# A two-layer encoder: shorter norm columns, and weight splits whose VectorE half is emitted one step later

## The chip, the core and the metric

One core of one Trainium2 chip runs the whole kernel. Its engines work side by side, each through its own instructions in order: TensorE (PE; its weight loads are listed as PEld), VectorE (DVE), ScalarE (ACT), GpSimd (POOL), and SyncE (SP), which issues most transfers. The metric is device time in microseconds (us), lower is better. The chip is asked for 2.4 GHz on TensorE; the profile shows the granted share of that, 1.00 or 0.50 (1.2 GHz).

## The reference

Two layers over 544 tokens of width 1024 (512 tokens of a new stream, 32 of a running one), all in float32. A layer is

```
h = rmsnorm(x);  proj = h @ w_in                # 5792 columns: conv gates, latent q, latent kv, rope key, two gates
y_a = (b * causal_conv3(c * xin)) @ w_conv_out
q = rmsnorm(q_lat) @ w_uq;  c = rmsnorm(ckv);  k, v = c @ w_ukv
y_b = chunk_causal_attention(q, k, v) @ w_attn_out
x = x + rmsnorm((sigmoid(g_a)*y_a + sigmoid(g_b)*y_b) @ w_merge)
x = x + rmsnorm((silu(gate) * up) @ w_down)     # gate, up = rmsnorm(x) @ w_gate_up, width 2816
```

Each rmsnorm multiplies a token by 1/sqrt(mean of squares + eps) and by a gain for each channel.

## The kernel before

Channels lie on the 128 partitions and tokens in the free dimension, in two halves of 272 tokens (hf 0 and 1). TensorE multiplies in fp32r, so each operand is split into a rounded high part and a low remainder, and a product takes three matmuls (`mm3`, lines 184 to 186: low weight first, then low input, then high by high).

**Weights.** A weight tile of 128 x 1024 is loaded by SP into one of two `raw` buffers. `split` then makes the high half with a ScalarE cast (L129) and the low half with a VectorE subtraction (L130), which waits for the cast and is the last to read `raw`. The result is one `w` tile: one of a ring of three, or a large block where `gate` is given. One weight tile against one half is a unit of 24 matmuls (`dense`), called a unit below; the last third of the down projection has 18.

**Order.** SP, POOL and TensorE always run in the order in which the program emits. VectorE and ScalarE do so in the program-ordered stages: the first projection pass of layer 0, and everything from the merge projection of a layer to the end of the first projection pass of the next. Elsewhere (attention, convolution, the other projections) a planner orders these two, and `prep` splits weights on the spot.

**The feed.** In the program-ordered stages from the merge projection on, weights come from a list, `feed`. `load_next` starts a load; `split_next` splits the oldest loaded tile; `claim`, ahead of the unit that uses a tile, forces what is missing. `tick` is called after each unit, behind the instructions that evict it: it splits the oldest tile if it was loaded at least two ticks ago and its buffer or gate allows, and then loads one more tile if fewer than two are loaded and not split. The stages that draw on it are, in order: the merge projection `mg` (8 tiles for half 0, the same tiles again for half 1), gate and up `gu` (4 pairs for half 0, again for half 1, then 18 pairs with both halves in turn), down `dn` (three tiles for each m; m = 0 to 4 with both halves, then half 0 of m = 5, 6, 7 and half 1 of m = 7, 6, 5), and in layer 0 the first pass of the next layer, `in` (8 tiles for half 0, then again for half 1).

**Norms.** `Acc` and `Acc2` add up squares. `rsqrt_cols` turns them into token columns with one-column matmuls (L237, two instructions for each of three blocks of 128 tokens), forms 1/sqrt with an integer start and three Newton steps on VectorE (L242 to L246), and multiplies the identity by each column into diagonal tiles (L251). `bcast` multiplies a matrix of ones by such a tile (L259, six instructions), which gives the factor on all partitions. `post_chain` does the residual and the norms around it in steps that `dense` takes in the middle and at the end of a unit; it runs after the last unit of each half of `mg` and `dn`. There are 24 calls of `bcast`: 14 in layer 0 and 10 in layer 1. The norms of q and kv are taken for both halves at once by `qk_norms`, near the end of the first pass.

Of the kernel before, what the change touches and what calls it, by code (L numbers as in the profile page):

```python
# [11 lines left out]
ALU = mybir.AluOpType  # L12
AX = mybir.AxisListType

P = 128
NL = 2
T = 544
TH = 272
# [5 lines left out]
EPS = 1e-6  # L24
QSCALE2 = 96.0
# [3 lines left out]
TB3 = (0, 128, 144)  # L29
# [4 lines left out]
def kernel(  # L34
# [25 lines left out]
    pe, dve, act, pool = nc.tensor, nc.vector, nc.scalar, nc.gpsimd  # L60
# [22 lines left out]
    def small(shape, dt=F32, s="s"):  # L83
        return sp.tile(shape, dt, tag="s", name=nm(s))

    def tiny(shape, s="y"):
        return sp.tile(shape, F32, tag="y", name=nm(s), bufs=16)
# [21 lines left out]
    def f32(ap):  # L109
        return ap.bitcast(F32)  # L110

    ident = const.tile([P, P], F32, name="ident")
    ones = const.tile([P, P], F32, name="ones")
# [14 lines left out]
    def split(hi, lo, src, eng_hi=None):  # L128
        act.copy(hi, src)  # L129
        dve.tensor_sub(lo, src, f32(hi))  # L130
# [13 lines left out]
    pre = {}  # L144
# [8 lines left out]
    feed, loaded, free, now = [], [], [0], [0]  # L153

    def load_next():
        key, src, width, gate = feed.pop(0)
        raw = raw_tile()
        nc.sync.dma_start(raw[:, :width], src)
        loaded.append((key, raw, width, gate, now[0]))

    def split_next():
        key, raw, width, gate, _ = loaded.pop(0)
        w = w_tile(gate is not None)
        split(w[:, 0, :width], w[:, 1, :width], raw[:, :width])
        pre[key] = w
        if gate is None:
            free[0] -= 1

    def tick():
        now[0] += 1  # L170
        if loaded and loaded[0][4] <= now[0] - 2 and (loaded[0][3]() if loaded[0][3] is not None else free[0] > 0):
            split_next()
        if feed and len(loaded) < 2:
            load_next()

    def claim(key):
        while key not in pre:
            if not loaded:
                load_next()
            split_next()  # L180
        return pre.pop(key)

    def mm3(ps, whi, wlo, xhi, xlo, first, last):
# [47 lines left out]
    def rsqrt_cols(accs):  # L231
        n = 3 * len(accs)
        ps = psd(n)
        v = tiny([P, 12], "v")[:, :n]
        for i, (acc, scale, eps) in enumerate(accs):
            for b, o in enumerate(TB3):
                pe.matmul(ps[:, 3 * i + b : 3 * i + b + 1], lhsT=acc.t[:, o : o + P], rhs=ones[:, 0:1], start=True, stop=True)  # L237
        for i, (acc, scale, eps) in enumerate(accs):
            dve.tensor_scalar(v[:, 3 * i : 3 * i + 3], ps[:, 3 * i : 3 * i + 3], scale, eps, op0=ALU.mult, op1=ALU.add)
        y = tiny([P, 12], "y")[:, :n]  # L240
        t = tiny([P, 12], "t")[:, :n]
        dve.tensor_scalar(y.bitcast(I32), v.bitcast(I32), -0.5, float(0x5F3759DF), op0=ALU.mult, op1=ALU.add)  # L242
        for _ in range(3):
            dve.tensor_mul(t, y, y)
            dve.scalar_tensor_tensor(t, t, -0.5, v, op0=ALU.mult, op1=ALU.mult)
            dve.scalar_tensor_tensor(y, t, 1.5, y, op0=ALU.add, op1=ALU.mult)  # L246
        out = []
        for i in range(len(accs)):
            d = small([P, TH], s="dg")
            for b, (o, a) in enumerate(((0, 0), (P, 0), (2 * P, 112))):  # L250
                dve.tensor_scalar_mul(d[:, o : min(o + P, TH)], ident[:, a:P], y[:, 3 * i + b : 3 * i + b + 1])  # L251
            out.append(d)
        return out

    def bcast(d, tag="v"):
        ps = bank(tag)[:, :TH]
        for o in (0, P, 2 * P):
            e = min(o + P, TH)
            pe.matmul(ps[:, o:e], lhsT=ones, rhs=d[:, o:e], start=True, stop=True)  # L259
        return ps  # L260

    FS = 1.0 / (NC * P)
# [168 lines left out]
    with tc.manual_schedule(engines=VEC):  # L431
        raw, w = raw_tile(True), w_tile(False)
# [20 lines left out]
    for l in range(NL):  # L453
# [47 lines left out]
                if m < 5:  # L501
                    (accq if m < 3 else acck)[hf].add(dst)

        qk = []

        def qk_norms():
            qk.extend(rsqrt_cols([(acck[0], 1.0 / 256, EPS), (acck[1], 1.0 / 256, EPS),
                                  (accq[0], QSCALE2 / 384, EPS * QSCALE2), (accq[1], QSCALE2 / 384, EPS * QSCALE2)]))

        if l == 0:  # L510
            pend = []

            def evict(n):
                for _ in range(n):
                    p1_evict(*pend.pop(0))

            after = {
                (0, 0): lambda: w3(3),
                (1, 0): lambda: (next(norm_a), scale_b(0), w3(4)),
                (2, 0): lambda: (scale_b(1), w3(5)),  # L520
                (3, 0): lambda: (next(norm_a), w3(6), evict(2)),
                (4, 0): lambda: (w3(7), evict(2), scale_b(2)),
                (5, 0): lambda: (scale_b(3), evict(2)),
                (6, 0): lambda: (evict(1), next(norm_b)),
                (7, 0): lambda: evict(1),
                (1, 1): lambda: (next(norm_b), next(norm_a)),
                (3, 1): lambda: (next(norm_b), evict(4)),
                (4, 1): lambda: evict(1),
                (5, 1): lambda: evict(1),
                (6, 1): lambda: (evict(1), qk_norms()),  # L530
                (7, 1): lambda: (evict(1), next(norm_b)),
            }

            def w3(m):
                if m == 5:
                    nc.sync.dma_start(cosT, rope[0])
                    nc.sync.dma_start(sinT, rope[1])
                fetch(("in", 0, m), w_in[0, m], 1024, True, m in (4, 5))

            with tc.manual_schedule(engines=VEC):  # L540
                for m, hf, ps in win_tiles(range(8), 8, raws):
                    pend.append((m, hf, ps))
                    if (m, hf) in after:
                        after[(m, hf)]()
        else:
            pend = []
            for m, hf, ps in win_tiles(range(8), 8, P1Src(h, raws)):
                pend.append((m, hf, ps))
                if hf == 0 or hf in sready:
                    while pend:  # L550
                        p1_evict(*pend.pop(0))
                tick()
                if (m, hf) == (6, 1):
                    qk_norms()
            while 1 not in h:
                step()
            while loaded:
                split_next()
            vec.__exit__(None, None, None)
        wide[0] = False  # L560

# [410 lines left out]
        def tail(units, key, widths, rhs, l, post_key, pre_l, pre_key, x_src, x_dst, gaps, outs):  # L972
            mres = [blk([P, NC, TH], F32, "m") for _ in range(2)]
            accs = [Acc(), Acc()]
            ws = {}
            left = [NC, NC]
            for n, (m, hf) in enumerate(units):
                left[hf] -= 1
                ps = psd(TH)
                for pi, wdt in enumerate(widths):  # L980
                    if (m, pi) not in ws:
                        ws[(m, pi)] = claim((key, m, pi))
                    dense(ps, ws[(m, pi)], rhs(hf, pi), wdt // P, first=pi == 0, last=pi == len(widths) - 1)
                    if (m, 1 - hf) not in units[n + 1 :] or (m, hf) == (5, 0) and len(widths) > 1:
                        del ws[(m, pi)]
                        if key == "mg" and m < 3 or key == "dn" and m != 6:
                            free[0] += 1
                    if pi < len(widths) - 1:
                        tick()
                done.add((key, m, hf))  # L990
                if accs[hf].q:
                    accs[hf].merge()
                accs[hf].square(ps)
                act.mul(mres[hf][:, m, :], ps, g(l, post_key, m))
                if left[hf] == 0:
                    accs[hf].merge()
                if (key, m, hf) == ("mg", 0, 1):
                    act.activation(tiny([P, 1]), ones[:, 0:1], AF.Silu)
                tick()
                if left[hf] == 0:  # L1000
                    xb = blk([P, NC, TH], F32, "xb")
                    for q in range(NW):
                        nc.gpsimd.dma_start(pair(xb, q), pair(x_src(hf), q))
                    chains.append(post_chain(pre_l, pre_key, mres[hf], accs[hf], xb, x_dst(hf), gaps[hf], hf, **outs[hf]))
# [29 lines left out]
        for _ in range(3):  # L1034
            load_next()
            split_next()
        load_next()
        now[0] += 1
        units = [(m, hf) for hf in range(2) for m in range(8)]
# [163 lines left out]
```

## Time and profile before

| | us |
|---|---|
| median of three runs | 2024.89 (2022.95 to 2026.08) |
| the profiled execution | 2026.63 |
| its span, first to last instruction | 2024.6 |
| TensorE busy | 1992.8 |
| VectorE busy | 1147.1 |
| ScalarE busy | 827.2 |

Busy time of TensorE is taken from matmul records whose ends are modelled and overlap. How long a stretch really takes is read from the distance between starts.

### The profile page before, as it was taken

How to read it: one execution, taken by the hardware profiler on the slowest of the kernel's cores; microseconds unless marked ns; L12 is line 12 of the kernel's file. 1: busy time of each engine (PE TensorE's matmuls, PEld its weight loads, DVE VectorE, ACT ScalarE, POOL GpSimd, SP SyncE). 2: the span in 40 equal slices, each digit the busy share in tenths (PEclk: the TensorE clock that was granted, in tenths of full speed). 3: DMA queues.
4: the chain of work that ended last, by engine and by line, in shares of the span. 5: the costliest groups of instructions: out<-in, count | busy, mean ns of one | idle time of the engine just before them, and what ended most of it. 6: DMA issues, size and time to landing. Idle time of an engine off the chain costs nothing.

```text
span 2024.6 us, 37375 instructions
## 1 busy us (share of the span) xinstructions
PE 1992.8 (98%) x15588; PEld 1970.8 (97%) x15588; DVE 1147.1 (57%) x2410; ACT 827.2 (41%) x1676; POOL 85.7 (4%) x212
## 2 busy tenths in 40 slices
PE   8999999999999999999999999999999999999997
PEld 8999999999999999999999999999999999999997
DVE  7877776534467444422668777864344664444234
ACT  5455555622353223222444555556123533222231
POOL 0100000000000000000100100100000000000000
PEclk9999999999999999999999999999999999999998
DMA  5122222222342222232532222222223412222233
GB/s 192 62 77 68 69 82 69 92 97 84 116 150 84 84 84 84 84 97 86 184 105 77 65 65 75 88 83 88 84 94 118 158 55 93 85 95 81 79 115 125
DMA packets 58890, 190.92 MB, mean 94 GB/s; under 512 B 7969, under 2 KB 9665, under 8 KB 58593
## 3 DMA queue, kind: packets, MB, share of 16 engines
q1 hardware_dynamic: 49104, 163.58, 24.1%
q0 software_dynamic: 8320, 22.66, 3.4%
q8 instruction: 122, 2.00, 0.4%
q10 hardware_dynamic: 1296, 2.29, 0.3%
q14 instruction: 48, 0.39, 0.1%
HBM read 174.11 MB, written 10.20 MB: 91 GB/s over the span
## 4 chain that ended last, share of the span: by engine, by line
PE 93%; DVE 4%; DMA 1%; ACT 1%; issue 1%; SPq 0%; DVEq 0%; ACTq 0%
PE ps_d L184 16%; PE ps_d L186 16%; PE ps_d L185 16%; PE ps_s L184 7%; PE ps_s L186 7%; PE ps_s L185 7%; PE ps_t L184 6%; PE ps_t L186 6%; PE ps_t L185 6%; PE ps_t L757 2%; DMA raw<-in_w_in 1%; PE ps_v L772 1%; PE ps_v L773 1%; DVE w L130 1%; ACT w L129 1%
## 5 line engine op out<-in xcount | busy, mean ns | idle before, releaser
L130 DVE TENSOR_TENSOR w<-raw,w 128x1024 fp32r<-128x1024 f32 (+4 forms) x317 | 363.8, 1148 | 433.5 <-ACT w L129 432.5
L129 ACT CAST w<-raw 128x1024 fp32r<-128x1024 f32 (+4 forms) x317 | 312.1, 986 | 263.3 <-PE ps_d L186 109.4
L184 PE MATMUL ps_d<-hh,w 128*128 128x272 f32 x1080 | 314.9, 292 | 1.3 <-DVE v L130 1.3
L185 PE MATMUL ps_d<-hl,w 128*128 128x272 f32 x1080 | 312.0, 289 | 0.8 <-DVE hl L314 0.8
L186 PE MATMUL ps_d<-hh,w 128*128 128x272 f32 x1080 | 312.1, 289 | 0.0
L184 PE MATMUL ps_d<-gh,w 128*128 128x272 f32 x704 | 205.9, 292 | 6.0 <-DVE w L130 6.0
L184 PEld LDWEIGHTS ps_d<-hh,w 128*128 128x128 f32 x1080 | 203.8, 189 | 3.0 <-PE ps_d L186 1.7
L185 PEld LDWEIGHTS ps_d<-hl,w 128*128 128x128 f32 x1080 | 203.5, 188 | 2.0 <-DVE hl L314 1.3
L186 PE MATMUL ps_d<-gh,w 128*128 128x272 f32 x704 | 204.5, 291 | 0.0
L185 PE MATMUL ps_d<-gl,w 128*128 128x272 f32 x704 | 203.5, 289 | 0.0
L186 PEld LDWEIGHTS ps_d<-hh,w 128*128 128x128 f32 x1080 | 203.1, 188 | 0.0
L184 PEld LDWEIGHTS ps_d<-gh,w 128*128 128x128 f32 x704 | 133.3, 189 | 6.5 <-DVE w L130 6.3
L184 PE MATMUL ps_s<-gh,w 128*128 128x272 f32 x464 | 136.9, 295 | 1.1 <-DVE w L130 1.1
L186 PE MATMUL ps_s<-gh,w 128*128 128x272 f32 x464 | 136.1, 293 | 0.0
L185 PE MATMUL ps_s<-gl,w 128*128 128x272 f32 x464 | 135.4, 292 | 0.0
L185 PEld LDWEIGHTS ps_d<-gl,w 128*128 128x128 f32 x704 | 133.6, 190 | 0.0
L186 PEld LDWEIGHTS ps_d<-gh,w 128*128 128x128 f32 x704 | 133.3, 189 | 0.0
L184 PE MATMUL ps_t<-gh,w 128*128 128x272 f32 x432 | 125.5, 290 | 0.0
L186 PE MATMUL ps_t<-gh,w 128*128 128x272 f32 x432 | 125.0, 289 | 0.0
L185 PE MATMUL ps_t<-gl,w 128*128 128x272 f32 x432 | 124.3, 288 | 0.0
L1051 ACT ACTIVATE sl<-sl 128x272 f32<-128x272 f32 x88 | 38.0, 432 | 183.2 <-DVE sl L1050 182.0
L1059 ACT CAST fh<-sl 128x272 fp32r<-128x272 f32 x88 | 36.9, 420 | 162.1 <-DVE sl L1057 162.1
(330 smaller groups left out, 5410.0 us busy)
## 6 DMA issues: line engine op xcount, KB each, us to landing
raw<-in_w_in SPq DMA_DIRECT2D x91, 512.0 KB, 3.2
raw<-in_w_gu SPq DMA_DIRECT2D x88, 512.0 KB, 3.2
raw<-in_w_mix SPq DMA_DIRECT2D x48, 512.0 KB, 3.2
raw<-in_w_dn SPq DMA_DIRECT2D x36, 512.0 KB, 3.5
raw<-in_w_dn SPq DMA_DIRECT2D x18, 384.0 KB, 3.0
raw<-in_w_b SPq DMA_DIRECT2D x16, 320.0 KB, 2.8
x_mid<-xb POOLq DMA_DIRECT2D x16, 272.0 KB, 2.3
xb<-x_mid POOLq DMA_DIRECT2D x16, 272.0 KB, 4.4
```

What stands on the lines that cost most here:

```text
L129: act.copy(hi, src)
L130: dve.tensor_sub(lo, src, f32(hi))
L184: pe.matmul(ps, lhsT=wlo, rhs=xhi, start=first, stop=False)
L185: pe.matmul(ps, lhsT=whi, rhs=xlo, start=False, stop=False)
L186: pe.matmul(ps, lhsT=whi, rhs=xhi, start=False, stop=last)
L757: pe.transpose(pt[:, o * P : o * P + P], probs[qt][:, kt * P : kt * P + P], ident)
L772: pe.matmul(out, lhsT=both, rhs=ptl[:, b, o : o + 256], start=kt == 0, stop=False)
L773: pe.matmul(out, lhsT=both, rhs=pth[:, b, o : o + 256], start=False, stop=kt == nkt - 1)
L1051: act.activation(sl, sl, AF.Silu)
L1059: act.copy(fh[:, i % 8, :], sl)
```

## The change

The diff has two halves. The norm half: `rsqrt_cols` takes two refinement steps, the first of higher order (seven instructions in place of nine), with other constants, and returns the columns themselves; no diagonal tiles are made; `bcast` transposes each column, read as 128 equal columns, with `pe.transpose`, three instructions in place of six; and `qk_norms` is called once for each half (layer 0 after units (4,1) and (6,1), layer 1 after (2,1) and (6,1)). The split half: in the feed, `split_next` emits only the ScalarE cast and puts the tile into `half`; `finish`, called at the head of the next tick or by `claim`, emits the VectorE subtraction. A tile in `half` counts against the limit of two in `tick`. The ticks inside the last unit group of a `tail` are left out.

```
     def split_next():
         key, raw, width, gate, _ = loaded.pop(0)
         w = w_tile(gate is not None)
-        split(w[:, 0, :width], w[:, 1, :width], raw[:, :width])
-        pre[key] = w
+        act.copy(w[:, 0, :width], raw[:, :width])
+        half.append((key, raw, w, width))
         if gate is None:
             free[0] -= 1
 
+    def finish():
+        while half:
+            key, raw, w, width = half.pop(0)
+            dve.tensor_sub(w[:, 1, :width], raw[:, :width], f32(w[:, 0, :width]))
+            pre[key] = w
+
     def tick():
         now[0] += 1
+        finish()
         if loaded and loaded[0][4] <= now[0] - 2 and (loaded[0][3]() if loaded[0][3] is not None else free[0] > 0):
             split_next()
-        if feed and len(loaded) < 2:
+        if feed and len(loaded) + len(half) < 2:
             load_next()
 
     def claim(key):
         while key not in pre:
-            if not loaded:
-                load_next()
-            split_next()
+            if not half:
+                if not loaded:
+                    load_next()
+                split_next()
+            finish()
         return pre.pop(key)
...
-        for _ in range(3):
-            dve.tensor_mul(t, y, y)
-            dve.scalar_tensor_tensor(t, t, -0.5, v, op0=ALU.mult, op1=ALU.mult)
-            dve.scalar_tensor_tensor(y, t, 1.5, y, op0=ALU.add, op1=ALU.mult)
-        out = []
-        for i in range(len(accs)):
-            d = small([P, TH], s="dg")
-            for b, (o, a) in enumerate(((0, 0), (P, 0), (2 * P, 112))):
-                dve.tensor_scalar_mul(d[:, o : min(o + P, TH)], ident[:, a:P], y[:, 3 * i + b : 3 * i + b + 1])
-            out.append(d)
-        return out
-
-    def bcast(d, tag="v"):
+        dve.tensor_mul(t, y, y)
+        dve.tensor_mul(t, t, v)
+        dve.scalar_tensor_tensor(u, t, -10.0 / 3.0, t, op0=ALU.add, op1=ALU.mult)
+        dve.scalar_tensor_tensor(y, u, 5.0, y, op0=ALU.add, op1=ALU.mult)
+        dve.tensor_mul(t, y, y)
+        dve.scalar_tensor_tensor(t, t, -27.0 / 1024.0, v, op0=ALU.mult, op1=ALU.mult)
+        dve.scalar_tensor_tensor(y, t, 0.5625, y, op0=ALU.add, op1=ALU.mult)
+        return [y[:, 3 * i : 3 * i + 3] for i in range(len(accs))]
+
+    def bcast(y, tag="v"):
         ps = bank(tag)[:, :TH]
-        for o in (0, P, 2 * P):
-            e = min(o + P, TH)
-            pe.matmul(ps[:, o:e], lhsT=ones, rhs=d[:, o:e], start=True, stop=True)
+        for b, o in enumerate(TB3):
+            pe.transpose(ps[:, o : o + P], y[:, b : b + 1].to_broadcast([P, P]), ident)
         return ps
...
-        def qk_norms():
-            qk.extend(rsqrt_cols([(acck[0], 1.0 / 256, EPS), (acck[1], 1.0 / 256, EPS),
-                                  (accq[0], QSCALE2 / 384, EPS * QSCALE2), (accq[1], QSCALE2 / 384, EPS * QSCALE2)]))
+        def qk_norms(hf):
+            qk[hf], qk[2 + hf] = rsqrt_cols([(acck[hf], 1.0 / 256, EPS), (accq[hf], QSCALE2 / 384, EPS * QSCALE2)])
...
-                    if pi < len(widths) - 1:
+                    if pi < len(widths) - 1 and n < len(units) - 1:
                         tick()
```

## Rows read from the trace of the kernel before

**Rows 1.** The page: busy time by engine, share of the span, instructions.

```profile
PE 1992.8 (98%) x15588; PEld 1970.8 (97%) x15588; DVE 1147.1 (57%) x2410; ACT 827.2 (41%) x1676; POOL 85.7 (4%) x212
```

**Rows 2.** Waits of PE: releaser, us in total, times, longest.

```profile
PE ps_v L259 <- DVE dg L251: 5.5, 2, 2.8
...
PE ps_d L237 <- DVE acc L224: 2.4, 2, 1.5
...
PE ps_d L185 <- DVE hl L314: 0.8, 2, 0.4
```

**Rows 3.** Waits of DVE, the first.

```profile
DVE w L130 <- ACT w L129: 432.5, 238, 9.9
```

**Rows 4.** Timeline of PE around a broadcast and a run of transposes: start, us, instruction.

```profile
583.78 0.73 PE L259 MATMUL ps_v<-dg,ones 128*128 128x128 f32 x6
584.36 0.37 PE L184 MATMUL ps_s<-mh,w 128*128 128x272 f32 x1
...
112.28 0.93 PE L757 MATMUL ps_t<-ident,pr 128*128 128x128 f32 x7
112.97 0.37 PE L184 MATMUL ps_d<-hh,w 128*128 128x272 f32 x1
```

**Rows 5.** Windows: stretch, us, busy time by engine, granted clock (PEclk), DMA share, GB/s.

```profile
61.90:65.30 3.40, 3.40 (x17) 3.40 (x16) 3.16 (x18) 0.00 (x0) 0.00 (x0) 0.50 0.00 0
1020.40:1024.40 4.00, 1.16 (x10) 0.97 (x10) 3.62 (x17) 2.02 (x5) 0.00 (x0) 1.00 0.58 206
1024.14:1028.76 4.62, 4.62 (x28) 4.62 (x27) 4.62 (x7) 1.24 (x2) 0.00 (x0) 0.63 0.43 138
1066.46:1072.05 5.59, 5.59 (x25) 5.59 (x26) 4.47 (x27) 0.00 (x0) 0.00 (x0) 0.50 0.00 0
```

**Rows 6.** Timeline of DVE at the end of the kernel.

```profile
2014.39 0.29 DVE L251 TENSOR_SCALAR dg<-ident,y 128x128 f32<-128x128 f32 x1
```

**Rows 7.** Timeline of PE at the end of the kernel.

```profile
2014.82 1.43 PE L259 MATMUL ps_v<-dg,ones 128*128 128x128 f32 x6 [2.63 <-DVE dg L251]
```

**Rows 8.** Timeline of ACT in the merge projection of layer 0.

```profile
554.56 0.40 ACT L215 ACTIVATE sq<-ps_s 128x272 f32<-128x272 f32 x1 [1.61 <-PE ps_s L186]
554.86 0.48 ACT L994 ACTIVATE m<-ps_s,gn 128x272 f32<-128x272 f32 x1
555.23 1.05 ACT L129 CAST w<-raw 128x1024 fp32r<-128x1024 f32 x1
557.59 0.40 ACT L215 ACTIVATE sq<-ps_t 128x272 f32<-128x272 f32 x1 [1.32 <-PE ps_t L186]
```

**Rows 9.** Timeline of DVE there.

```profile
556.31 1.23 DVE L130 TENSOR_TENSOR w<-raw,w 128x1024 fp32r<-128x1024 f32 x1 [2.07 <-ACT w L129]
...
563.56 0.43 DVE L224 TENSOR_TENSOR acc<-acc,sq 128x272 f32<-128x272 f32 x1
```

**Rows 10.** The page: weight loads, KB each, median us from issue to landing.

```profile
raw<-in_w_mix SPq DMA_DIRECT2D x48, 512.0 KB, 3.2
```

**Rows 11.** Timeline of ACT near the end of half 0 of the down projection of layer 0.

```profile
966.54 1.05 ACT L129 CAST w<-raw 128x1024 fp32r<-128x1024 f32 x1 [1.81 <-DMA raw<-in_w_dn]
...
971.55 0.40 ACT L215 ACTIVATE sq<-ps_s 128x272 f32<-128x272 f32 x1 [1.16 <-PE ps_s L186]
```

**Rows 12.** Timeline of ACT in the first pass of layer 1.

```profile
1017.30 0.38 ACT L500 COPY lat<-ps_s 128x272 f32<-128x272 f32 x1
1017.71 0.43 ACT L215 ACTIVATE sq<-lat 128x272 f32<-128x272 f32 x1
```

**Rows 13.** Timeline of DVE there.

```profile
1019.75 1.23 DVE L130 TENSOR_TENSOR w<-raw,w 128x1024 fp32r<-128x1024 f32 x1 [1.09 <-ACT w L129]
1020.89 0.15 DVE L239 TENSOR_SCALAR v<-ps_d 128x3 f32<-128x3 f32 x1
...
1028.45 0.72 DVE L335 TENSOR_TENSOR m<-m,ps_v 128x544 f32<-128x544 f32 x1
```

**Rows 14.** Timeline of PE there.

```profile
1023.48 0.81 PE L259 MATMUL ps_v<-dg,ones 128*128 128x128 f32 x6 [2.84 <-DVE dg L251]
```

More of the change, by code (lines that the diff above doesn't have):

```diff
@@ L159, in load_next @@
         loaded.append((key, raw, width, gate, now[0]))
+    half = []
     def split_next():
@@ L241, in rsqrt_cols @@
         t = tiny([P, 12], "t")[:, :n]
+        u = tiny([P, 12], "u")[:, :n]
         dve.tensor_scalar(y.bitcast(I32), v.bitcast(I32), -0.5, float(0x5F3759DF), op0=ALU.mult, op1=ALU.add)
-        for _ in range(3):
-            dve.tensor_mul(t, y, y)
-            dve.scalar_tensor_tensor(t, t, -0.5, v, op0=ALU.mult, op1=ALU.mult)
-            dve.scalar_tensor_tensor(y, t, 1.5, y, op0=ALU.add, op1=ALU.mult)
-        out = []
-        for i in range(len(accs)):
-            d = small([P, TH], s="dg")
-            for b, (o, a) in enumerate(((0, 0), (P, 0), (2 * P, 112))):
-                dve.tensor_scalar_mul(d[:, o : min(o + P, TH)], ident[:, a:P], y[:, 3 * i + b : 3 * i + b + 1])
-            out.append(d)
-        return out
-    def bcast(d, tag="v"):
+        dve.tensor_mul(t, y, y)
[7 more added lines that the diff above has]
+    def bcast(y, tag="v"):
         ps = bank(tag)[:, :TH]
-        for o in (0, P, 2 * P):
-            e = min(o + P, TH)
-            pe.matmul(ps[:, o:e], lhsT=ones, rhs=d[:, o:e], start=True, stop=True)
+        for b, o in enumerate(TB3):
+            pe.transpose(ps[:, o : o + P], y[:, b : b + 1].to_broadcast([P, P]), ident)
         return ps
@@ L502, in p1_evict @@
                     (accq if m < 3 else acck)[hf].add(dst)
-        qk = []
-        def qk_norms():
-            qk.extend(rsqrt_cols([(acck[0], 1.0 / 256, EPS), (acck[1], 1.0 / 256, EPS),
-                                  (accq[0], QSCALE2 / 384, EPS * QSCALE2), (accq[1], QSCALE2 / 384, EPS * QSCALE2)]))
+        qk = {}
+        def qk_norms(hf):
+            qk[hf], qk[2 + hf] = rsqrt_cols([(acck[hf], 1.0 / 256, EPS), (accq[hf], QSCALE2 / 384, EPS * QSCALE2)])
         if l == 0:
@@ L527 @@
                 (3, 1): lambda: (next(norm_b), evict(4)),
-                (4, 1): lambda: evict(1),
+                (4, 1): lambda: (evict(1), qk_norms(0)),
                 (5, 1): lambda: evict(1),
-                (6, 1): lambda: (evict(1), qk_norms()),
+                (6, 1): lambda: (evict(1), qk_norms(1)),
                 (7, 1): lambda: (evict(1), next(norm_b)),
@@ L552 @@
                 tick()
+                if (m, hf) == (2, 1):
+                    qk_norms(0)
                 if (m, hf) == (6, 1):
-                    qk_norms()
+                    qk_norms(1)
             while 1 not in h:
@@ L558 @@
                 split_next()
+            finish()
             vec.__exit__(None, None, None)
@@ L1036 @@
             split_next()
+        finish()
         load_next()
```

## The prediction, made before the changed kernel was run

> **What bounds the kernel now.** Read the busy times first: TensorE is busy for 1992.8 of 2024.6 us, with 15588 matmuls [rows 1]. Everything else matters only where TensorE waits, runs at the lower clock, or is given more or fewer instructions. So read its waits second. Those that the change touches are small: 5.5 us in two waits for the diagonal tiles of a norm (2.8 the longest), 2.4 for the summed squares in front of a norm, 0.8 for the low half of a normed input [rows 2]. Third, VectorE: it waits 432.5 us for ScalarE's cast in front of the weight subtraction [rows 3]. That is the wait at which the split half aims, but on an engine that is idle for over 40% of the span it is worth only what TensorE loses by it. Fourth, the windows with the granted clock: it is 0.50 in 61.90 to 65.30 and in 1066.46 to 1072.05, both behind the 24 one-column matmuls of the q and kv norms, and falls behind 1020.40 to 1024.40, where TensorE was busy for 1.16 us of 4.00 [rows 5].
>
> A unit of 24 matmuls takes 3.03 us (two evictions, 554.56 and 557.59, [rows 8]), 0.126 each.
>
> **Norm half, broadcast.** Six instructions took 583.78 to 584.36, 0.58 us; seven transposes took 112.28 to 112.97, 0.10 each [rows 4], so three take 0.30. The trace has no transpose that reads one column 128 times over. If that read costs nothing the gain is 0.28, and if it eats the gain it is 0. I take 0.28, from the nearest row. Of the 24 calls one lies in the tail; 23 x 0.28 = 6.4 us off TensorE's own time (bounds 0 to 6.4). The Trainium skill ("TensorE: Matmul & The Clock Gate", Part 4: PE-mode transpose) says that a 128 x 128 transpose took about 275 ns in one kernel. Paid three times over, that would be 0.83 per broadcast, and the term 23 x 0.25 = 5.8 us lost instead of 6.4 gained; the 0.10 between starts in [rows 4] speaks against that reading.
>
> **Norm half, VectorE.** Two small instructions (0.2 each) and three diagonal tiles for each norm go. In the tail nothing covers them: the first diagonal tile starts at 2014.39 [rows 6] and TensorE at 2014.82 [rows 7], of which 0.3 goes; with 0.4 for the two and half of the 1.43 of the broadcast, 1.4 us. In layer 0 the twelve diagonal tiles of the q and kv norms stand on VectorE ahead of the normed input that TensorE awaits; those 0.8 us [rows 2] go. Elsewhere VectorE's saving lies beside matmuls and is worth nothing.
>
> **Norm half, clock.** The 24 one-column matmuls become 12 and 12, some units apart. Six of them with the 1.5 us wait in front [rows 2], near 1015, did not lower it (1.00 in 1020.40 to 1024.40, [rows 5]), so I take it that 12 don't. What comes back: a unit that took 5.59 us at 0.50 (1066.46, layer 1) takes 3.03, 2.6; in 61.90 to 65.30 there ran 17 matmuls in place of 27 [rows 5], 10 x 0.126 = 1.3. The third fall cost one unit 4.62 - 3.03 = 1.6 [rows 5] and goes with its wait (below). Sum 5.5, bounds 0 and 5.5.
>
> **Split half, the supply.** This is where I differ from what the edit says. A `raw` tile now counts against the limit of two until its subtraction is emitted. Before, a tick split one tile and loaded one: a tile per tick. Now follow it: a tick that casts A still counts A and B, and loads nothing; the next finishes A, casts B, loads C; the next finishes B and loads D, but casts nothing, because C is only one tick old. Two tiles in three ticks. Where both halves use a tile in turn (`gu`, most of `dn`) the demand is one in two, and I found casts at the same tick as before or with two units to spare. Three stretches ask for one tile per tick.
>
> *Place n* is the point ahead of unit n. Merge, half 0: tiles 5, 6, 7 were cast at places 3, 4, 5; now at 4, 5 and 7. The cast at place 7 stands on ScalarE behind the eviction of unit 6, and unit 7 on TensorE behind both halves. The price from [rows 8, 9]: square to cast 0.67 (554.56 to 555.23), cast to subtraction 1.08 (556.31), subtraction 1.23, and some 0.2 for the last matmul to drain: 3.2 us of idle TensorE. Tiles 5 and 6, cast one unit ahead, need 3.2 against the unit's 3.03: 0.2 late. The loads themselves are no bound: they take 3.2 us [rows 10] and start as soon as a buffer is free. 3.4 per layer, 6.8.
>
> Down, m = 6 and 7 of half 0 (six tiles, places 0 to 5): cast before at -2, -1, 0, 1, 2, 3, now at -1, 1, 2, 3, 4, 5. Before, the cast of (7,0) could start at 966.54, ahead of the eviction at 971.55 [rows 11]; now it stands behind that eviction: 3.2 again. (6,1) is 0.2 late; (7,1) and (7,2) have no eviction in front. 3.4 per layer, 6.8.
>
> First pass of layer 1, half 0: tiles 1 to 7 were cast at places -4 to 2, and now, with the inner ticks of the last units gone too, at 0, 1, 3, 4, 5, 6, 7. Tile 1: 0.3. Tile 2: its subtraction now stands on VectorE behind the sum of the unit just ended: 0.2 + 0.38 copy + 0.43 square [rows 12] + 0.44 sum + 1.23 [rows 9] = 2.7. Tile 3: 0.2 + 0.38 + 0.41 + 1.05 + 1.23 = 3.3. Tiles 4 and 5 the same with one 0.72 instruction of the post chain in front [rows 13]: 4.0 each. Tiles 6 and 7 have no square in front: 2.9 each. Sum 20.1. Against that goes what is lost there now: the column arithmetic at 1020.89 stood behind a subtraction at 1019.75 [rows 13], so TensorE waited 2.84 at 1023.48 [rows 14], and 1.5 for the squares [rows 2]: 4.3. Net 15.8.
>
> **Clock behind the new waits.** Each long wait is like 1020.40 to 1024.40, after which one unit lost 1.6. Ten such waits give 0 to 16 us; I take 7 (3 of the 4 lone ones, 4 of the 6 in the pass), 11.2.
>
> **The sum.** + 6.8 + 6.8 + 15.8 + 11.2 - 5.5 - 6.4 - 0.8 - 1.4 = + 26.5 us. The profiled execution took 2026.63 (span 2024.6 and 2.0 around it), 1.7 above the median of 2024.89; on the median that is 2051.4, so 2051. With the bounds of clock and broadcast: 2036 to 2062.
>
> **Rivals.** (1) *The feed never runs dry*, because casts are not held behind evictions and the two-in-three rate never decides. For it: the casts in [rows 11] do run ahead. Against: in [rows 8] the cast follows the eviction. The gains stand alone, 6.4 + 0.8 + 1.4 + 5.5 + 4.3 = 18.4: 2006. It decides if TensorE shows no wait for L129's tile at place 7 of the merge. (2) *Only the pass starves*; the four lone waits are covered: 26.5 - 13.6 - 4.8 = 8.1, 2033. (3) *The clock stays at 0.50 through the starved pass*, since TensorE works less than half of it: six units lose 2.6 each in place of 6.4 in all, and all four lone waits lose 1.6: + 37, 2062. (4) *As (2), and no clock falls in the pass*: + 1.7, about 2026, no change.
>
> **Chances.** Mine 0.56, (1) 0.14, (2) 0.12, (3) 0.12, (4) 0.06. Within 0.2% (4 us) is what a measurement can't tell from no change. Faster 0.14, same 0.06, slower 0.80. The range takes in (2) and most of (3): 2028 to 2063; the likeliest case's own is 2036 to 2062.
>
> **What would show it.** TensorE's waits for the weight subtraction rise to some 30 us, with waits of about 3 us ahead of the eighth merge unit and the 37th of the down projection in each layer, and six ahead of units of layer 1's first pass; broadcasts last 0.30; the clock is full behind the q and kv norms and falls in the first pass. If those long waits are missing, the supply argument is wrong and the time is near 2006; if they are there and the total is under 2030, the clock term or the gains are mis-sized.

## The result and the profile after

The changed kernel took 2055.65 us (median of 4 runs, 2054.06 to 2059.71) against 2024.72 for the kernel before (4 runs, 2022.95 to 2026.08): ratio 1.0156 with the interval 1.0139 to 1.0174, 30.9 us slower. The profiled execution took 2054.99 us, its span is 2053.0, 28.4 more than before. Its lines have moved: the three matmuls of a product are L195 to L197, the feed's cast is L166 and its subtraction L174, the subtraction of a split in one piece L130, the broadcast L267, the columns' sums L248.

The page's busy times answer to [rows 1], and the two groups of VectorE's subtractions (busy us, mean ns, idle before and what ended it) to [rows 3].

```profile
PE 1994.3 (97%) x15516; PEld 1969.1 (96%) x15516; DVE 1126.3 (55%) x2318; ACT 825.3 (40%) x1676; POOL 86.1 (4%) x212
...
L174 DVE TENSOR_TENSOR w<-raw,w 128x1024 fp32r<-128x1024 f32 (+1 forms) x168 | 199.7, 1192 | 209.0 <-ACT w L166 208.9
L130 DVE TENSOR_TENSOR w<-raw,w 128x1024 fp32r<-128x1024 f32 (+4 forms) x149 | 163.0, 1094 | 138.5 <-ACT w L129 137.2
```

TensorE is busy 1.5 us longer and idle 26.9 us longer (span less busy: 58.7 against 31.8). VectorE's wait for the casts did fall, from 432.5 to 208.9 + 137.2 = 346.1. So the loss is TensorE's waiting, and what the norm half saved has to have been eaten inside the busy time. The waits of TensorE in the kernel after (releaser, us in total, times, longest) say for what it waits:

```profile
PE ps_d L195 <- DVE w L174: 13.8, 5, 3.7
PE ps_s L195 <- DVE w L174: 8.7, 3, 3.1
PE ps_t L195 <- DVE w L174: 8.5, 3, 3.1
...
PE ps_v L267 <- DVE y L261: 1.9, 1, 1.9
...
PE ps_d L196 <- DVE hl L322: 0.8, 2, 0.4
PE ps_d L196 <- DVE qn L130: 0.8, 1, 0.8
```

Eleven waits, 31.0 us, for the weight subtraction of the feed. Before there were none of this kind: TensorE's waits for a weight subtraction (6.0 and 1.1 us) all lie in the first 13 us, outside the feed. Those for the broadcast's operand fell from 5.5 to 1.9, the tail's; the low half in layer 0 is as it was; a wait for `qn` in the attention of layer 0 is new. The timeline of TensorE (start, us, instruction, in brackets the idle time before it) has four of the eleven by themselves, alike in both layers: in front of the eighth merge unit (573.52, 1601.42) and of the 37th unit of the down projection (976.09, 2003.99). In the first pass of layer 1 seven follow each other.

```profile
573.52 0.39 PE L195 MATMUL ps_t<-mh,w 128*128 128x272 f32 x1 [3.06 <-DVE w L174]
...
976.09 0.39 PE L195 MATMUL ps_d<-fh,w 128*128 128x272 f32 x1 [3.06 <-DVE w L174]
...
1017.31 0.39 PE L195 MATMUL ps_d<-hh,w 128*128 128x272 f32 x1 [1.38 <-DVE w L174]
...
1023.80 0.39 PE L195 MATMUL ps_s<-hh,w 128*128 128x272 f32 x1 [2.55 <-DVE w L174]
...
1030.23 0.39 PE L195 MATMUL ps_t<-hh,w 128*128 128x272 f32 x1 [2.80 <-DVE w L174]
...
1037.20 0.59 PE L195 MATMUL ps_d<-hh,w 128*128 128x272 f32 x1 [3.68 <-DVE w L174]
...
1046.02 0.59 PE L195 MATMUL ps_s<-hh,w 128*128 128x272 f32 x1 [3.13 <-DVE w L174]
...
1053.50 0.60 PE L195 MATMUL ps_t<-hh,w 128*128 128x272 f32 x1 [2.68 <-DVE w L174]
...
1061.99 0.40 PE L195 MATMUL ps_d<-hh,w 128*128 128x272 f32 x1 [2.68 <-DVE w L174]
```

By the distance from the last matmul's start to the next one's, less the usual 0.126, each lone wait costs 3.22 us, and those of the pass cost 1.54, 2.71, 2.97, 3.84, 3.32, 2.84 and 2.98, together 20.2.

Why a lone wait lasts 3.2 us is read from ScalarE ahead of 573.52. It answers to [rows 8], where the tile that was cast at 555.23 was one needed later; here unit 7 itself awaits the tile cast at 571.17.

```profile
570.50 0.40 ACT L226 ACTIVATE sq<-ps_s 128x272 f32<-128x272 f32 x1 [2.25 <-PE ps_s L197]
570.80 0.48 ACT L1004 ACTIVATE m<-ps_s,gn 128x272 f32<-128x272 f32 x1
571.17 1.04 ACT L166 CAST w<-raw 128x1024 fp32r<-128x1024 f32 x1
```

The cast stands behind the eviction of the unit just ended, the subtraction (572.24, 1.22 us) behind the cast, and TensorE behind both. In the pass the chain is the same with the in-order queues of both engines in it. Tile 3 on VectorE: the subtraction stands behind a chain instruction (as [rows 13] had one) and a sum, and then waits another 0.41 us for its cast, so here the cast still decides:

```profile
1027.46 0.72 DVE L343 TENSOR_TENSOR m<-m,ps_v 128x544 f32<-128x544 f32 x1 [3.71 <-PE ps_v L267]
1028.10 0.43 DVE L235 TENSOR_TENSOR acc<-acc,sq 128x272 f32<-128x272 f32 x1
1028.95 1.22 DVE L174 TENSOR_TENSOR w<-raw,w 128x1024 fp32r<-128x1024 f32 x1 [0.41 <-ACT w L166]
```

The windows (us, busy times, granted clock, DMA share, GB/s) answer to [rows 5]: the clock is full where the q and kv norms now lie, and falls behind three of the four lone waits (575.00, 1602.40, 2005.20; not behind 976) and behind four of the pass.

```profile
59.00:66.00 7.00, 7.00 (x60) 7.00 (x59) 4.93 (x19) 1.30 (x4) 1.35 (x2) 1.00 0.00 0
...
575.00:578.41 3.41, 3.41 (x18) 3.41 (x17) 0.00 (x0) 0.22 (x1) 0.00 (x0) 0.50 0.29 113
976.00:979.41 3.41, 3.32 (x26) 3.32 (x27) 1.17 (x2) 0.00 (x0) 0.00 (x0) 1.00 0.61 172
1035.80:1042.63 6.83, 5.43 (x24) 5.43 (x24) 5.41 (x9) 3.03 (x7) 1.08 (x2) 0.50 0.44 161
```

18 matmuls fit where at full clock there fit 27. At 0.50 they start 0.227 apart (21 steps, 1037.59 to 1042.35) and otherwise 0.126, so 0.44 of the busy time in such a stretch is lost: 12.5 us over the seven stretches (busy 3.41, 5.43, 3.39, 5.81, 3.41, 3.41, 3.41), against 6.0 over the three of before (3.40, 3.41, 6.83).

The broadcast of [rows 4] is now 0.25 us from its first transpose to the next matmul:

```profile
1005.60 0.49 PE L267 MATMUL ps_v<-ident,y 128*128 128x128 f32 x3
1005.85 0.38 PE L195 MATMUL ps_s<-fh,w 128*128 128x272 f32 x1
```

### The profile page after: what moved, and what is told of

Its sections match the earlier page's. It is cut to its first block, busy times and chain, and to the rows that moved or that the text cites. A ratio compares the mean times of both kernels' runs of the same rounds, so it can differ in the third digit from the quotient of the medians.

```text
span 2053.0 us, 37142 instructions
## 1 busy us (share of the span) xinstructions
PE 1994.3 (97%) x15516; PEld 1969.1 (96%) x15516; DVE 1126.3 (55%) x2318; ACT 825.3 (40%) x1676; POOL 86.1 (4%) x212
## 4 chain that ended last, share of the span: by engine, by line
PE 93%; DVE 4%; ACT 2%; DMA 1%; issue 1%; SPq 0%; DVEq 0%; ACTq 0%
PE ps_d L195 16%; PE ps_d L197 16%; PE ps_d L196 16%; PE ps_s L195 7%; PE ps_s L197 7%; PE ps_s L196 7%; PE ps_t L195 6%; PE ps_t L197 6%; PE ps_t L196 6%; PE ps_t L767 2%; PE ps_v L782 1%; PE ps_v L783 1%; DMA raw<-in_w_in 1%; DVE w L174 1%; DVE w L130 1%
## 5 line engine op out<-in xcount | busy, mean ns | idle before, releaser
L195 PE MATMUL ps_d<-hh,w 128*128 128x272 f32 x1096 | 321.8, 294 | 9.1 <-DVE w L174 7.7
L197 PE MATMUL ps_d<-hh,w 128*128 128x272 f32 x1096 | 318.5, 291 | 0.0
L174 DVE TENSOR_TENSOR w<-raw,w 128x1024 fp32r<-128x1024 f32 (+1 forms) x168 | 199.7, 1192 | 209.0 <-ACT w L166 208.9
L130 DVE TENSOR_TENSOR w<-raw,w 128x1024 fp32r<-128x1024 f32 (+4 forms) x149 | 163.0, 1094 | 138.5 <-ACT w L129 137.2
L195 PEld LDWEIGHTS ps_d<-hh,w 128*128 128x128 f32 x1096 | 208.3, 190 | 11.5 <-DVE w L174 8.5
L129 ACT CAST w<-raw 128x1024 fp32r<-128x1024 f32 (+4 forms) x149 | 140.7, 944 | 179.4 <-PE ps_d L197 84.5
L195 PE MATMUL ps_d<-gh,w 128*128 128x272 f32 x704 | 206.1, 293 | 6.5 <-DVE w L130 6.5
L166 ACT CAST w<-raw 128x1024 fp32r<-128x1024 f32 (+1 forms) x168 | 170.9, 1022 | 103.1 <-DMA raw<-in_w_gu 22.5
L197 PEld LDWEIGHTS ps_d<-hh,w 128*128 128x128 f32 x1096 | 208.0, 190 | 0.0
L197 PE MATMUL ps_d<-gh,w 128*128 128x272 f32 x704 | 204.6, 291 | 0.0
L195 PEld LDWEIGHTS ps_d<-gh,w 128*128 128x128 f32 x704 | 133.6, 190 | 6.9 <-DVE w L130 6.8
L195 PE MATMUL ps_t<-gh,w 128*128 128x272 f32 x464 | 135.0, 291 | 0.0
L197 PE MATMUL ps_t<-gh,w 128*128 128x272 f32 x464 | 134.3, 289 | 0.0
L196 PE MATMUL ps_t<-gl,w 128*128 128x272 f32 x464 | 133.6, 288 | 0.0
L197 PEld LDWEIGHTS ps_d<-gh,w 128*128 128x128 f32 x704 | 133.4, 189 | 0.0
L195 PE MATMUL ps_s<-gh,w 128*128 128x272 f32 x432 | 125.4, 290 | 0.7 <-DVE w L130 0.7
L197 PE MATMUL ps_s<-gh,w 128*128 128x272 f32 x432 | 125.0, 289 | 0.0
L196 PE MATMUL ps_s<-gl,w 128*128 128x272 f32 x432 | 124.4, 288 | 0.0
```

The source lines that it names most:

```text
L166: act.copy(w[:, 0, :width], raw[:, :width])
L174: dve.tensor_sub(w[:, 1, :width], raw[:, :width], f32(w[:, 0, :width]))
L195: pe.matmul(ps, lhsT=wlo, rhs=xhi, start=first, stop=False)
L196: pe.matmul(ps, lhsT=whi, rhs=xlo, start=False, stop=False)
L197: pe.matmul(ps, lhsT=whi, rhs=xhi, start=False, stop=last)
```

## The experiments

The theory to test: the waits come from the feed's limit, which counts a tile that is cast and not yet subtracted, so that the feed brings two tiles in three ticks. The rival in most of them: the later VectorE half does harm by itself, whatever the supply. Each edit is shown against the kernel it starts from.

**One half each.** e1_norm_only is the kernel after with the old feed:

```diff
-        act.copy(w[:, 0, :width], raw[:, :width])
-        half.append((key, raw, w, width))
+        split(w[:, 0, :width], w[:, 1, :width], raw[:, :width])
+        pre[key] = w
...
-        if feed and len(loaded) + len(half) < 2:
+        if feed and len(loaded) < 2:
...
-                    if pi < len(widths) - 1 and n < len(units) - 1:
+                    if pi < len(widths) - 1:
```

> The norm half alone, the feed as before. Supply theory (the norm half gains, the split half loses through the two-tiles-in-three-ticks supply): the changed kernel's trace shows broadcasts of 0.25 us in place of 0.58, so 23 x 0.33 = 7.6; the tail 1.25 shorter; the clock full behind the q and kv norms, 3.9 + 0.4. The waits near layer 1's first pass (1.5 and 2.8 to 3.0) stay or shrink by under 1 us. About 13 us faster than before, 2009 to 2015. Rival (the norm half is what makes the change slow, for instance through transposes that cost as much as ones-matmuls or through the longer life of the columns): 2024 or more.

e2_split_only is the kernel after with the norms of before:

```diff
-            pe.transpose(ps[:, o : o + P], y[:, b : b + 1].to_broadcast([P, P]), ident)
+            pe.matmul(ps[:, o:e], lhsT=ones, rhs=d[:, o:e], start=True, stop=True)
...
-        def qk_norms(hf):
+        def qk_norms():
```

> The split half alone, the norms as before. Supply theory: all of the new waits (four of 3.2 us, seven of 1.5 to 4.2 in the first pass of layer 1) and the clock falls behind them, without the norm half's gains: 2055.7 + 13 = 2066 to 2072. Rival (the halves hurt only together): near 2040 or below.

Measured: e1 2014.25 us, ratio 0.9961 (0.9947 to 0.9975), and repeated as e1b_norm_only 2013.36, 0.9947 (0.9934 to 0.9961); e2 2068.55, 1.023 (1.0215 to 1.0246). The before kernel beside e1 and e2 took 2023.40, beside e1b 2024.41. e1 and e2 lie in their expected ranges, though e1's gain is less than the 13 us forecast. So the norm half gains 9 to 11 us and the split half costs 45; the sum, 34 to 36, is a few us above the 30.9 of both together. All of the loss is in the split half.

**The limit without the count.** e3_uncounted changes one condition of the kernel after:

```diff
-        if feed and len(loaded) + len(half) < 2:
+        if feed and len(loaded) < 2:
```

> The changed kernel with one condition put back: a tile whose subtraction is pending no longer counts against the limit of two loads. The VectorE half is still emitted one tick later. Supply theory: one tile per tick again, so the four lone waits of 3.2 us go and of the waits in layer 1's first pass at most one or two short ones remain (inner ticks of the last units are still left out, so the last tiles of the pass come late, 1 to 2 us); the older waits of 1.6 and 3.0 us there go as well. 2003 to 2013. Rival (the later VectorE half itself makes TensorE wait, since the subtraction queues behind evictions): the lone waits stay, 2045 or more.

Measured: 2020.07 us, 0.9982 (0.9971 to 0.9992). The four lone waits are gone, which shows that the count made them. The size missed by 7 us and more, and the trace says why: waits that neither the kernel before nor the supply theory has. The longest, 3.46 us from 1033.02, lies in the first pass of layer 1. ScalarE there, and then VectorE:

```profile
1030.32 1.04 ACT L166 CAST w<-raw 128x1024 fp32r<-128x1024 f32 x1
```

```profile
1033.44 0.72 DVE L302 TENSOR_TENSOR sqw<-sqw,sqw 128x544 f32<-128x544 f32 x1
1034.98 0.44 DVE L235 TENSOR_TENSOR acc<-sq,sq 128x272 f32<-128x272 f32 x1 [0.82 <-ACT sq L226]
1035.34 1.22 DVE L174 TENSOR_TENSOR w<-raw,w 128x1024 fp32r<-128x1024 f32 x1
```

The tile that TensorE awaits was cast by 1031.36. Its subtraction, emitted a step later, starts at 1035.34, behind the sum (1034.98) of a unit that first had to end; the clock falls behind this wait. The rival's own sign (the lone waits stay, 2045 or more) did not come, but its mechanism, a subtraction that queues behind other work, is there as a second cost.

**The ticks.** The edit also drops the ticks inside the last unit of a stage. e6_uncounted_ticks is e3 and e7_counted_ticks is the kernel after, both with these ticks back; e5_norm_skip is e1 without them (the line the other way):

```diff
-                    if pi < len(widths) - 1 and n < len(units) - 1:
+                    if pi < len(widths) - 1:
```

> The norm half with the feed as before, but without the ticks inside the last unit group of a tail (the one piece of the split half's code that takes work out of VectorE's way). Theory: the three waits that the norm half alone still has near layer 1's first pass (1.6, 1.7 and 0.5 us, with one clock fall behind them) stood behind the casts and subtractions of two tiles that these ticks emit; they go, and at one tile per tick the pass keeps up. 2.5 to 5 us faster than the norm half alone, 2009 to 2012. Rival (the pass then starves as in the changed kernel): a wait of 2 us or more for a subtraction in the pass, 2014 or more.

> The changed kernel with the pending tile not counted and the inner ticks of the last unit group put back: supply as before, VectorE half one tick later. Theory: of the waits that were left without the count (1.9 and 3.5 us in layer 1's first pass, with two clock falls, and two of 1.3 to 1.5 us ahead of a broadcast in the gate and up stage of both layers) the first two go, the two ahead of the broadcasts stay, since they come from subtractions that now stand in front of the norm columns. 2011 to 2016, so no better than the norm half alone. Rival (the missing ticks had no part in the waits of the pass): 2018 or more.

> The changed kernel with the inner ticks put back and the count kept. It splits the loss in the pass: the count alone leaves the four lone waits of 3.2 us (with their clock falls) and about three waits in the pass in place of seven, one of them long. 2036 to 2048. Rival (the count alone causes the whole loss in the pass): 2053 or more; rival (the missing ticks alone cause it): no waits over 1 us in the pass, 2030 or less.

Measured: e5 2012.74, 0.9947 (0.9932 to 0.9962), 0.7 us above its range; e6 2021.35, 0.999 (0.998 to 0.9999), a miss and in its rival's range; e7 2042.48, 1.0094 (1.0079 to 1.0109), as expected, with three waits in the pass (1.16, 7.22 and 2.84 us by the spacing). In e6 the two waits that should have gone have others in their place (2.05 and 4.48): where the limit does not count the pending tile, bringing the ticks back does not help. e5 was run again as e5b_norm_skip beside e1b:

> The norm half alone once more, beside the next two on one chip in five rounds, to tell the versions apart that lie within 2 us of each other: about 2014, as in the first three rounds.

> The norm half without the inner ticks of the last unit group, in five rounds. Theory (the waits of 1.7 and 0.5 us that it takes away are worth their time): 1 to 3 us faster than the norm half alone. Rival (another wait or clock fall takes their place): within 1 us of it.

e5b took 2011.54, 0.9941 (0.9928 to 0.9953). It is the fastest version, ahead of both kernels; its 1.8 us on e1b are not settled, since the intervals overlap. The table gives the difference from the kernel before, run beside each, in us; "later half" is the VectorE half emitted one step later:

```
feed                                  inner ticks kept     dropped
old (both halves at once)             -9.2, -11.1          -11.2, -12.9
later half, limit without the count   -2.6                 -3.3
later half, limit with the count      +18.5                +30.9 (the change)
```

Down the columns: the later half alone costs some 7 to 10 us; the count 21 with the ticks and 34 without. Across: the ticks are worth 12 when the feed is short and, at most, about 2 the other way when it is not. In e7 the lone waits are still 3.22 each, so the ticks' part lies in the pass.

How the later half costs where supply is full, e6 shows. The rows are ScalarE's there, then TensorE's, then the wait of the DMA queue from 1000 to 1021:

```profile
1017.66 1.04 ACT L166 CAST w<-raw 128x1024 fp32r<-128x1024 f32 x1 [4.28 <-DMA raw<-in_w_in]
1018.61 0.39 ACT L226 ACTIVATE sq<-ps_s 128x272 f32<-128x272 f32 x1
```

```profile
1019.53 1.44 PE L248 MATMUL ps_d<-ones,acc 128*128 128x1 f32 x6 [4.32 <-DVE acc L235]
```

```profile
SPq L158 <- DVE w L174: 16.5, 3, 10.1
```

The longest of these waits is 10.1 us; in e1, from 995 to 1015, it is 3.7. A load waits for its `raw` buffer, which comes free with the subtraction of the tile before the last; the subtraction later makes the load later, the cast waits 4.28 us for it, and behind the cast stands the square that the norm awaits. In e1 the same square (1008.61) started 0.7 us before the start of the last matmul of the unit ahead of the norm (1009.30); here it starts 3.7 after it (1014.92).

**The clock behind the waits.** e4_filled is the kernel after with 24 matmuls more ahead of the starved units (the eighth merge and 37th down unit of each layer, tiles 2 to 7 of the pass). They write a bank that the unit then overwrites, so they only keep TensorE working:

```diff
+    def spare(ps, x, n):
+        for k in range(n):
+            pe.matmul(ps, lhsT=x[0][:, k % 6, 0:P], rhs=x[0][:, k % 6, :], start=k == 0, stop=k == n - 1)
...
+                            spare(ps, src[hf], 24)
...
+                        spare(ps, rhs(hf, pi), 24)
```

> The changed kernel with 24 extra matmuls into the bank that the unit behind them overwrites, ahead of the eighth merge unit and the 37th down unit in each layer and ahead of tiles 2 to 7 of layer 1's first pass: TensorE computes something unused for about 3.0 us in place of waiting 2.7 to 3.8. Theory that the waits cost twice, once as idle time and once through the clock behind them (about 13 us of the total): the clock stays full, the waits are hidden in the extra matmuls, 2040 to 2048. Rival (the clock has no part in it and what I booked there is work): no gain or slower, 2055 or more.

Measured: 2045.47, 1.0114 (1.0099 to 1.0129). Doing more work made the kernel some 9 us faster (+22.1 against its before, where the change has +30.9; the intervals of the two ratios do not overlap). The mean granted clock is 0.997 or 0.998 in all four of its runs, and 0.988 to 0.991 in the four of the kernel after. The pass, window 1012 to 1064, and the filling of one wait on TensorE:

```profile
1012.00:1064.00 52.00, 48.40 (x377) 47.46 (x377) 25.93 (x49) 21.20 (x39) 2.69 (x5) 1.00 0.27 93
```

```profile
1033.18 3.17 PE L214 MATMUL ps_d<-hh 128*128 128x272 f32 x24
...
1037.03 0.39 PE L198 MATMUL ps_d<-hh,w 128*128 128x272 f32 x1 [0.68 <-DVE w L174]
```

The clock is full throughout the pass. The 240 extra matmuls (30.2 us at 0.126) and what is left of the waits (1.81, 0.82 and 1.01 by the spacing, at tiles 1, 4 and 5) take about 34 us, where the waits took 33.1. So the clock behind the new waits cost some 9 us, and the waits themselves the rest.

**The q and kv norms.** e8_qk_halves is the kernel before with these norms in two parts of 12 columns:

```diff
-                (6, 1): lambda: (evict(1), qk_norms()),
+                (6, 1): lambda: (evict(1), qk_norms(1)),
...
-                    qk_norms()
+                    qk_norms(1)
```

> The kernel before with one edit: the norms of q and kv taken for each half, so 12 and 12 one-column matmuls in place of 24. Theory that the run of 24 was what lowered the clock: it stays full there in both layers, 3.9 + 0.4 us, 2018 to 2020.5. Rival (the clock falls are due to something else near the end of the pass): 2022 or more, with the clock at 0.50 as before.

Measured: 2022.31, 0.9993 (0.9983 to 1.0002). By the time this is inconclusive, and the expected size missed. In its trace both falls behind these norms are gone (the stretches are those of [rows 5], a little longer):

```profile
62.00:66.00 4.00, 4.00 (x34) 4.00 (x33) 3.59 (x20) 0.00 (x0) 0.00 (x0) 1.00 0.00 0
1060.00:1066.00 6.00, 6.00 (x51) 6.00 (x51) 6.00 (x13) 3.63 (x8) 0.00 (x0) 1.00 0.00 0
```

That is not enough to make the run of 24 the cause. e2 has the norms of before, and so the same run in both layers, and nothing that it changes lies ahead of the first. Its runs on TensorE, then the windows behind them:

```profile
58.04 2.73 PE L248 MATMUL ps_d<-ones,acc 128*128 128x1 f32 x24
...
1096.35 2.73 PE L248 MATMUL ps_d<-ones,acc 128*128 128x1 f32 x24
```

```profile
62.00:66.00 4.00, 4.00 (x34) 4.00 (x33) 3.77 (x21) 0.00 (x0) 0.16 (x1) 1.00 0.00 0
1100.00:1105.00 5.00, 5.00 (x42) 5.00 (x41) 4.59 (x27) 0.00 (x0) 0.00 (x0) 1.00 0.01 3
```

The clock is full behind both. So the run of 24 was followed by a fall in the trace of before and not in that of e2, and what decides it stays open. e8's ten runs have a mean granted clock of 0.995 to 0.997 and the 19 of the kernel before beside them 0.994 to 0.996, so parting the run may make falls rarer; that is not shown.

The span fell by 4.0 us (2020.6). Of this 1.6 lie in the wait in front of a broadcast near 1024, which took 1.39 by the spacing and 3.00 before. In layer 0 gaps in front of the matmuls that read the normed input took part of the gain: at 68.03, 69.34, 70.80 and 72.67, 0.41 to 0.59 each, where before had two of 0.56 and 0.58.

**A longer gap in the chain.** e9_gap is e5 with two pauses of the chain behind the down projection shifted:

```diff
-    GD = ((1, 3, 5, 3, 0, 0), (2, 3, 7, 4, 1, 4))
+    GD = ((1, 3, 6, 2, 0, 0), (2, 3, 7, 4, 1, 4))
```

> The version above with the second norm of half 0's post chain in the down projection taken half a unit later and its broadcast where it was (pauses 5, 3 become 6, 2). Theory: its trace has a wait of 1.6 us for the summed squares (near 991) and a clock fall behind it; the squares are ready 1.6 us late and half a unit is 1.1 to 1.5 us, so the wait shrinks to under 0.6, and 2 to 3 us go: 2009 to 2011. Rival (the column arithmetic is then late for the broadcast): a wait there in place of the other, 2012 or more.

Measured: 2017.71, 0.997 (0.9959 to 0.998), 6 us worse than e5b; the theory fell and its rival held. TensorE waited 8.49 us at 1004.19 for the norm's columns, and VectorE shows on what:

```profile
992.74 2.09 DVE L130 TENSOR_TENSOR w<-raw,w 128x768 fp32r<-128x768 f32 x2
1001.17 1.23 DVE L130 TENSOR_TENSOR w<-raw,w 128x1024 fp32r<-128x1024 f32 x1 [6.35 <-ACT w L129]
1002.32 0.15 DVE L239 TENSOR_SCALAR v<-ps_d 128x3 f32<-128x3 f32 x1
```

The columns' arithmetic, 0.15 us an instruction, was emitted one place later and so stood behind a subtraction whose cast waited 6.55 us for its load; in e5b it starts at 994.72, ahead of that subtraction (1001.09). In e3 and e6 too TensorE pays for what stands ahead in an engine's order: in e3 a sum ahead of the subtraction on VectorE, in e6 a cast ahead of the square on ScalarE.

## Why the prediction was right

The forecast was 2051, the time 2055.65, inside the likeliest case's own range; the case itself happened. On the profiled spans the difference is 28.4 us against the 26.5 predicted. That it is so close is in part luck: errors of 0.5 to 1.3 us in single terms nearly cancel, the clock term was a choice, and four runs of the kernel after alone span 5.7 us. The range of this case was also added up wrongly: with the bounds given for the terms (0 to 16 for the clock behind the waits, 0 to 5.5 for that behind the norms, 0 to 6.4 for the broadcasts) it is 2040 to 2068, not 2036 to 2062. Step by step:

- *Supply, two tiles in three ticks.* Right. The lone waits lie at the four places named, 3.22 us each where 3.2 was worked out from the rows of eviction, cast and subtraction, 12.9 in all. e3 shows that the count makes them. The four smaller pieces of 0.2 cannot be seen among the usual spacings.
- *First pass.* Sum right, 20.2 against 20.1, because two errors in it nearly cancel. Tile 1 cost 1.54 and not 0.3: its cast (1014.95) stood behind eight instructions of the new layer's normed input (from 1009.86) and an eviction on ScalarE, which I had not counted in its queue. Tile 5 cost 3.32 and not 4.0: no chain instruction stood in front of its subtraction. Nor did one at tile 4, which cost 3.84 as forecast: VectorE was idle there, and the chain instructions stood on ScalarE, in front of the eviction. The old waits of 4.3 are gone as predicted (1.63 and 3.0 by the spacing, 4.6). Tile 4 on ScalarE, then on VectorE:

```profile
1033.58 0.64 ACT L294 ACTIVATE sqw<-xb 128x544 f32<-128x544 f32 x1
1034.13 0.36 ACT L508 COPY lat<-ps_t 128x272 f32<-128x272 f32 x1
...
1034.86 1.03 ACT L166 CAST w<-raw 128x1024 fp32r<-128x1024 f32 x1
```

```profile
1035.92 1.23 DVE L174 TENSOR_TENSOR w<-raw,w 128x1024 fp32r<-128x1024 f32 x1 [2.39 <-ACT w L166]
```

- *The pass's cause.* Half right. I put all of it down to supply, in which the missing ticks have 12 us by e7. With full supply the later half still costs 7 to 10 us of its own by e3 and e6, so undoing the count does not give back the whole loss; for e3 I had expected that it would.
- *Clock behind the new waits.* 12.5 against 11.2 by the busy times, and 3 of the 4 lone waits and 4 of the pass, as chosen. It was a choice between 0 and 16; e4 bears out that the clock takes part, with some 9. That the count of falls came out exactly is luck: in e7 all four lone waits, 3.22 us each there too, are followed by one (mean granted clock 0.68 to 0.74 in the 5 to 8.5 us behind each).
- *Clock behind the q and kv norms.* The sign came: full in both layers. The mechanism is not shown: by e2's trace a run of 24 need not lower the clock, so the 5.5 was counted from falls of one execution that another need not have. In that execution all three falls of before cost 6.0 by their busy time.
- *Broadcasts.* 0.33 saved each and not 0.28: 23 x 0.33 = 7.6 against 6.4. Reading one column 128 times over cost nothing that can be seen. The 275 ns that the Trainium skill ("TensorE: Matmul & The Clock Gate", Part 4: PE-mode transpose) gives for a transpose in one kernel are the length of one record here (272), not what one costs in a row of them: three take 0.25 us from the first start to the next matmul.
- *Low half in layer 0.* Failed: 0.8 predicted, 0 gained. The twelve diagonal tiles stood ahead of the normed input on VectorE, but between the two stands an eviction, and without the tiles it waits 1.29 us for TensorE's unit to end instead:

```profile
63.53 0.41 DVE L483 TENSOR_TENSOR ue<-cs,ps_t 128x240 f32<-128x240 f32 x1 [1.29 <-PE ps_t L197]
63.85 0.18 DVE L484 TENSOR_TENSOR ue<-cs,ps_t 128x32 f32<-128x32 f32 x1
63.95 1.35 DVE L315 TENSOR_TENSOR hf<-x,rr 128x544 f32<-128x544 f32 x2
```

- *Tail.* 1.25 against 1.4: from the last long matmul to the end 13.26 us where it was 14.5.
- *Not foreseen.* The wait for `qn` in layer 0's attention, 1.0 by the spacing. e1 has it too (1.0 at 85.98), so it comes with the norm half.

The measured terms add up to 12.9 + 20.2 - 4.6 + 12.5 - 6.0 - 7.6 - 1.25 + 1.0 = 27.2; 1.2 of the 28.4 stay open.

Of the rivals, the first (the feed never runs dry) and the two with covered lone waits fell with the four waits of 3.22. The third (0.50 through the whole pass) fell with windows of 0.69 (1034 to 1048) and 0.71 (1048 to 1064).

## What to carry over

Follow a prefetch by its limit, tick by tick: an instruction that is emitted a step later holds its buffer a step longer, and a limit that counts the held one turns one tile per tick into two in three, here at 2.7 to 3.8 us for each tile that comes a whole chain late, and 1.5 to 2.6 more where the clock falls behind it. On an engine that works in order, emitting a 1.2 us instruction later saves its engine's waiting (here TensorE gained nothing by it) and may make it stand in front of the next short instruction that the busiest engine needs. Ask of each engine's long wait whether the bounding engine loses anything by it: of VectorE's 432.5 us in [rows 3] 86 went, and TensorE was idle 26.9 us longer. And before a fall of the clock is put down to what ran ahead of it, look for the same instructions in other traces: some have no fall.

## What was not expected of the hardware

Twelve one-column matmuls in a row (58.97 to 60.22, 1.25 us) left the clock full; 24 were followed by a fall to 0.50 in the trace of the kernel before and by none in e2's. Of four waits alike to 0.01 us (3.06 by the brackets) three were followed by a fall of the clock and one, at 976.09, was not, while in e7 all four were; what makes the difference was not tried. And in e4 1.5% more matmuls (15756 against 15516) made the kernel some 9 us faster, nearly all of it by the clock.
